# The attention's product with the values in two matmuls for each tile of keys in place of three

## The chip, the cores and the metric

One core of one Trainium2 chip runs one kernel: two layers of a transformer block with sandwiched feed-forward parts and a mixed attention and pooling part, for 256 tokens of an image (x) and 256 tokens of context (ctx), all in float32 arithmetic. The metric is the device time in microseconds of one execution, as the median of several runs; less is better.

## The reference, cut to what matters

```python
def neighbourhood_attention(q, k, v, kc, vc, rpb, rows):      # x's queries
    ...
    scores = jnp.concatenate([s_loc.reshape(...), s_ctx], axis=-1)   # 256 local and 256 context keys
    p = jax.nn.softmax(scores, axis=-1).astype(v.dtype)
    ...
    o = einsum('bhrqkc,brkchd->brqhd', p_loc, v_blk) + einsum('bhrqk,bkhd->brqhd', p_ctx, vc)

def context_attention(q, k, v):                               # ctx's queries, first layer alone
    p = jax.nn.softmax(sc, axis=-1).astype(v.dtype)
    return jnp.einsum('bhqk,bkhd->bqhd', p, v).reshape(b, l, h * dh)

def token_mix(hx, hc, ...):
    ...
    out_x = jnp.concatenate([na_x, pool_x], axis=-1) @ w_out
```

There are 8 heads of 64 channels. In the kernel the local window covers all 256 image tokens (the window of 8 rows is cut to the 4 rows of 64 that there are), with the bias and mask added to the scores. So each head multiplies probabilities of 256 queries by 512 keys with 512 x 64 values, and in the first layer those of 256 context queries by 256 keys with 256 x 64 values.

## The kernel before, in words

**Precision.** Float32 operands of a matmul are held as two parts, a high one in the faster format fp32r and a low one, the rest. `split` (L535) makes them: a ScalarE copy into the high part, and a VectorE subtraction for the low part. `mm3` (L530) multiplies two such pairs with three matmuls: high by high, high by low, low by high.

**Stages.** Each layer is a feed-forward part (ffn), the token mix, and a second feed-forward part. In the token mix, `v_tile` (L957) makes the values of 128 tokens in a PSUM bank (pv) and splits them into V, a tile of 128 tokens by two token tiles by high and low by 512 channels. Keys and queries of a pair of heads come from `k_part` and `q_part`; `roped` turns them (a ScalarE copy, a VectorE shuffle, a GpSimd and a VectorE product with the rotary tables ropet, a VectorE sum, all in a tile rp), and the queries end in qa, the keys in kb. `pooled` is the pooling part, with a chain of GpSimd additions (U, dd) and a product py. The output projection (pd) multiplies mix, the eight blocks of 128 channels from heads and pooling, with the weights w_out; `close` (L784) norms a tile of 128 tokens, adds it to x and turns it into the next part's input.

**One head** (`head`, L1011; pr is the pair, 0 to 3, and e the head in it): scores (pS, and pC for the context's queries), softmax in the tiles sx and sc, transposes of the probabilities into a bank pp, a split into pT (or pT2), and `back` (L1021), which is the change's place. It runs over the tiles of 128 keys, four for x and two for the context. The stationary operand is a 128 x 128 block of V, the high or the low part of both heads of the pair; the moving one is the probabilities' high or low part, 128 keys by 256 queries. The bank po holds 128 channels by 256 queries, of which only the 64 rows of this head are used; `split` brings these to mix's high (mhi) and low (mlo) part. There are 16 such products in layer 0 (8 heads, x and context) and 8 in layer 1.

**Weights.** A stream brings 1 MB pieces by DMA into raw; ScalarE and VectorE split each into two tiles named w (w_big in the profile), one tile ahead of their use.

**Order.** Nothing is written out by hand. The code records its operations, and `Recorder.order` (L293) places them one at a time on five clocks, with prices by `price` (L208), with buffers taken from five pools (16 large slots "big", 10 "wk", 8 PSUM banks, 2 raw, 24 small) and a small bonus for an operation marked with haste. Within an engine the operations then run strictly in the order found. Every changed operation can therefore move all that come after it, on all engines. All recorded operations carry the line of the issuing helper, L376; the profile tells them apart by the names of tiles.

Of the kernel before, what the change touches and what calls it, by code (L numbers as in the profile page):

```python
# [17 lines left out]
P = 128  # L18
D = 1024
KD = D // P  # L20
S = 256
# [372 lines left out]
def tile_dit_block(  # L394
# [25 lines left out]
    nc = rec  # L420
# [530 lines left out]
    def token_mix(l, nxt):  # L951
# [5 lines left out]
        def v_tile(t, wv4):  # L957
            pv = bank("pv")
            tk = slice(t * P, (t + 1) * P)
            for k in range(KD):  # L960
                w = wv4[k // 2]
                hh = H["now"][k // 4]
                c = slice((k % 2) * 512, (k % 2 + 1) * 512)
                mm3(pv, (hh[0][:, k % 4, tk], hh[1][:, k % 4, tk]), (w[:, 0, c], w[:, 1, c]), k == 0, k == KD - 1)
            if t % 2 == 0:
                V[t // 2] = slot([P, 2, 2, 512], "v")
            split(V[t // 2][:, t % 2, 0, :], V[t // 2][:, t % 2, 1, :], pv)

# [42 lines left out]
        def head(pr, e, qk, bx):  # L1011
            qa, kb = qk
            hp = slice(e * 64, (e + 1) * 64)
            vc = slice(pr * P, (pr + 1) * P)
            mhi, mlo = mixed(pr)
# [4 lines left out]

            def back(src, keys, co):  # L1021
                po = bank("po")
                for i, t in enumerate(keys):
                    vt = V[t // 2]
                    mm3(
                        po[:, 0:S],
                        (vt[:, t % 2, 0, vc], vt[:, t % 2, 1, vc]),
                        (src[:, 0, i, :], src[:, 1, i, :]),
                        i == 0,
                        i == len(keys) - 1,  # L1030
                    )
                split(mhi[hp, co], mlo[hp, co], po[hp, 0:S])

# [45 lines left out]
            for t in range(2):  # L1079
# [4 lines left out]
                split(pT[:, 0, :, t * P : (t + 1) * P], pT[:, 1, :, t * P : (t + 1) * P], ppv)  # L1084
            back(pT, (0, 1, 2, 3), XS)
            if full:
                pp = bank("pp")
                for t in range(2):
                    for kt in range(2):
                        o = kt * S + t * P  # L1090
                        nc.tensor.transpose(pp[:, o : o + P], sc[:, t, kt * P : (kt + 1) * P], ident)
                pT2 = wtile([P, 2, 2, S], "pT2", F32R)
                split(pT2[:, 0], pT2[:, 1], pp.rearrange("p (k q) -> p k q", k=2))
                back(pT2, (2, 3), CS)
            rec.haste = 0.0
# [264 lines left out]
```

## Time and profile before

| | |
|---|---|
| median of 3 runs | 1678.48 us (1678.24 to 1678.59) |
| profiled execution | 1679.59 us |
| its span, first to last instruction | 1677.8 us |
| mean granted TensorE clock | 0.994 |
| matmuls of the values' product (po) | 240, in two parts of the span: 455.8 to 569.0 us and 1392.5 to 1468.1 us |

In the profile, PE is TensorE's matmul and PEld its weight load, DVE is VectorE, ACT ScalarE, POOL GpSimd. `out<-in` names the tiles by the program's names. A busy time counts an instruction from its start to its modelled end, so that matmuls in a pipeline overlap. In the timeline, `xN` on a row merges N instructions, and a bracket at its end gives the idle time before it and what ended that. In the chain of waits each row is a stretch of time in which that engine was the one waited for.

### The profile page before, as it was taken

The page shows a single profiled execution, that of the slowest core. Times are in us where ns is not written, and L with a number is a line of the kernel's source. Part 1 is how long each engine was busy: PE and PEld are TensorE (multiplying, and loading weights), DVE is VectorE, ACT ScalarE, POOL GpSimd, SP SyncE. Part 2 cuts the span into 40 slices and gives each one's busy share as a digit, 9 for nine tenths or more (in the row PEclk, how much of TensorE's full clock was granted, in tenths as well). Part 3 has the DMA queues.
Part 4 walks back from the last instruction along what each step waited for, and adds up shares of the span by engine and source line. Part 5 has one row for each costly group of instructions (what it writes and reads, how often), then busy time and mean ns, then how long its engine had stood idle before and what let it go on. Part 6 is the DMA issues. An engine that isn't in the chain of part 4 may idle for free.

```text
span 1677.8 us, 21889 instructions
## 1 busy us (share of the span) xinstructions
PE 1637.7 (98%) x8390; PEld 1374.9 (82%) x8390; DVE 1132.5 (67%) x1610; ACT 689.1 (41%) x1222; POOL 214.7 (13%) x264
## 2 busy tenths in 40 slices
PE   6999999999999999999999999999999999899998
PEld 4988888888877798888888898888888888779997
DVE  7997777556789689867745498533343488975664
ACT  7433222225566562232222273142222367664442
POOL 1022111102133211210110012100000022210000
PEclk9999999999999999999999999999999999999999
DMA  9467656621222426765554248432232212355551
GB/s 373 175 232 247 223 181 210 211 100 60 96 67 93 151 101 211 247 230 204 179 184 163 100 161 302 165 126 88 88 128 97 93 60 98 124 195 195 203 195 58
DMA packets 98953, 269.00 MB, mean 160 GB/s; under 512 B 9425, under 2 KB 39329, under 8 KB 87073
## 3 DMA queue, kind: packets, MB, share of 16 engines
q1 hardware_dynamic: 98848, 267.60, 45.3%
q8 instruction: 66, 1.08, 0.3%
q14 instruction: 39, 0.31, 0.1%
HBM read 251.80 MB, written 1.09 MB: 151 GB/s over the span
## 4 chain that ended last, share of the span: by engine, by line
PE 85%; DVE 5%; ACT 5%; POOL 2%; issue 1%; DMA 1%; SPq 0%; DVEq 0%; POOLq 0%; ACTq 0%
PE pd_ps L376 26%; PE pu_ps L376 25%; PE pg_ps L376 25%; PE pk_ps L376 2%; PE pv_ps L376 2%; ACT n_wk L376 2%; DVE w_big L376 1%; POOL rs_st L376 1%; PE pq_ps L376 1%; DMA w_big<-in_wmod_dram 1%; PE pt_ps L376 1%; ACT w_big L376 1%; PE po_ps L376 1%; ACT sx_wk L376 1%; ACT yg_wk L376 1%
## 5 line engine op out<-in xcount | busy, mean ns | idle before, releaser
L376 DVE TENSOR_TENSOR w_big<-raw_raw,w_big 128x1024 fp32r<-128x1024 f32 x312 | 389.0, 1260 | 167.1 <-ACT w_big L376 166.6
L376 PE MATMUL pu_ps<-h_big,w_big 128*128 128x512 f32 (+1 forms) x2400 | 474.9, 351 | 0.0
L376 PE MATMUL pg_ps<-h_big,w_big 128*128 128x512 f32 (+1 forms) x2208 | 439.8, 353 | 1.4 <-ACT h_big L376 1.4
L376 PEld LDWEIGHTS pu_ps<-h_big,w_big 128*128 128x128 f32 x2400 | 389.8, 188 | 62.2
L376 PE MATMUL pd_ps<-w_big,g_big 128*128 128x512 f32 x1848 | 431.2, 394 | 0.0
L376 ACT ACTIVATE w_big<-raw_raw 128x1024 fp32r<-128x1024 f32 x312 | 322.3, 1053 | 261.1 <-PE pd_ps L376 95.3
L376 PEld LDWEIGHTS pg_ps<-h_big,w_big 128*128 128x128 f32 x2208 | 361.4, 189 | 61.1 <-ACT h_big L376 1.8
L376 PEld LDWEIGHTS pd_ps<-w_big,g_big 128*128 128x128 f32 x1848 | 346.3, 188 | 78.9
L376 DVE SCALAR_TENSOR_TENSOR acc_wk<-wm_wk,csil,acc_wk 128x1024 f32<-128x1024 f32 x196 | 247.0, 1293 | 42.2 <-DMA wm_wk<-in_wmod_dram 42.0
L376 ACT ACTIVATE g_big<-tt_wk 128x512 fp32r<-128x512 f32 (+1 forms) x84 | 49.1, 585 | 314.3 <-DVE tt_wk L376 314.2
L376 POOL TENSOR_TENSOR part_wk<-part_wk 128x512 f32<-128x512 f32 (+2 forms) x84 | 93.4, 1113 | 504.8 <-DMA part_wk<-acc_wk 405.9
L376 ACT ACTIVATE tt_wk<-pg_ps 128x512 f32<-128x512 f32 (+1 forms) x86 | 47.3, 550 | 163.0 <-PE pg_ps L376 134.3
L376 DVE TENSOR_TENSOR tt_wk<-tt_wk,pu_ps 128x512 f32<-128x512 f32 (+1 forms) x86 | 54.0, 628 | 77.2 <-PE pu_ps L376 76.8
L376 POOL TENSOR_SCALAR rs_st<-sq_st 128x1 f32<-128x1 f32 x24 | 7.6, 315 | 731.9 <-ACT n_wk L376 731.8
L376 DVE SCALAR_TENSOR_TENSOR tt_wk<-tt_wk,pg_ps 128x512 f32<-128x512 f32 (+1 forms) x86 | 53.9, 627 | 69.5 <-ACT tt_wk L376 69.1
L376 DVE TENSOR_TENSOR g_big<-tt_wk,g_big 128x512 fp32r<-128x512 f32 (+1 forms) x84 | 54.1, 644 | 30.7 <-ACT g_big L376 30.7
L376 PE MATMUL pd_ps<-w_big,mix_big 128*128 128x512 f32 x288 | 71.8, 398 | 0.5 <-DVE mix_big L376 0.5
L376 DVE TENSOR_TENSOR y_big<-y_big,pd_ps 128x512 f32<-128x512 f32 x56 | 37.7, 683 | 45.1 <-PE pd_ps L376 45.0
L376 PEld LDWEIGHTS pd_ps<-w_big,mix_big 128*128 128x128 f32 x288 | 52.9, 190 | 12.1 <-DVE mix_big L376 1.2
L376 PE MATMUL pk_ps<-h_big,w_big 128*128 128x512 f32 (+1 forms) x240 | 50.0, 350 | 0.0
L376 PE MATMUL pv_ps<-w_big,h_big 128*128 128x512 f32 x192 | 47.0, 397 | 0.0
L376 PEld LDWEIGHTS pk_ps<-h_big,w_big 128*128 128x128 f32 x240 | 37.7, 188 | 5.1
(136 smaller groups left out, 1219.1 us busy)
## 6 DMA issues: line engine op xcount, KB each, us to landing
raw_raw<-in_wgu_dram SPq DMA_DIRECT2D x84, 1024.0 KB, 4.9
wm_wk<-in_wmod_dram SPq DMA_DIRECT2D x128, 512.0 KB, 6.5
raw_raw<-in_wdn_dram SPq DMA_DIRECT2D x44, 1024.0 KB, 5.0
part_wk<-acc_wk SPq DMA_DIRECT2D x224, 64.0 KB, 2.5
raw_raw<-in_wkq_dram SPq DMA_DIRECT2D x8, 1024.0 KB, 4.9
raw_raw<-in_wout_dram SPq DMA_DIRECT2D x8, 1024.0 KB, 4.8
w_big<-in_wmod_dram SPq DMA_DIRECT2D x7, 1024.0 KB, 11.7
gb_wk<-grow SPq DMA_DIRECT2D x10, 512.0 KB, 5.4
```

The costliest lines, as they stand in the source:

```text
L376: getattr(getattr(nc, op.engine), op.method)(*[self.real(a) for a in op.args], **{k: self.real(a) for k, a in op.kw.items()})
```

## The change

V's tile gets another layout: for each token tile and each pair of heads four blocks of 64 channels, in the order high part of head 0, low of head 0, low of head 1, high of head 1. The two blocks of one head are now side by side and serve as one stationary operand of 128 columns. One matmul with the probabilities' high part and one with their low part then give the high part's product in 64 rows of po and the low part's product in the other 64; both halves of the bank are used, and the product of low by low, left out before, is included. For head 0 the high block lies in rows 0 to 63, for head 1 in rows 64 to 127, which are the rows of the head in mix.

The two halves have to be added. ScalarE copies the high half of po to mhi, as before, and the other half to a work area tmp, across the partitions; VectorE subtracts mhi from po's high half into tmp in place of mlo; GpSimd adds the two pieces of tmp into mlo. The work area is the head's own sx or sc, whose probabilities have been transposed by then; it stays taken until that add.

```diff
-                V[t // 2] = slot([P, 2, 2, 512], "v")
-            split(V[t // 2][:, t % 2, 0, :], V[t // 2][:, t % 2, 1, :], pv)
+                V[t // 2] = slot([P, 2, 4, 4, 64], "v")
+            vt = V[t // 2][:, t % 2]
+            split(vt[:, :, 0:4:3, :], vt[:, :, 1:3, :], pv.rearrange("p (r e d) -> p r e d", r=4, e=2))
...
-            def back(src, keys, co):
+            def back(src, keys, co, tmp):
+
                 po = bank("po")
                 for i, t in enumerate(keys):
-                    vt = V[t // 2]
-                    mm3(
-                        po[:, 0:S],
-                        (vt[:, t % 2, 0, vc], vt[:, t % 2, 1, vc]),
-                        (src[:, 0, i, :], src[:, 1, i, :]),
-                        i == 0,
-                        i == len(keys) - 1,
-                    )
-                split(mhi[hp, co], mlo[hp, co], po[hp, 0:S])
+                    vt = V[t // 2][:, t % 2, pr, 2 * e : 2 * e + 2, :].rearrange("p b d -> p (b d)")
+                    for part in range(2):
+                        mm(po[:, 0:S], vt, src[:, part, i, :], i == 0 and part == 0, i == len(keys) - 1 and part == 1)
+                nc.scalar.activation(mhi[hp, co], po[hp, 0:S], AF.Copy)
+                nc.scalar.activation(tmp[hp, 0:S], po[HEADS[1 - e], 0:S], AF.Copy)
+                nc.vector.tensor_sub(tmp[hp, S : 2 * S], po[hp, 0:S], mhi[hp, co])
+                nc.gpsimd.tensor_add(mlo[hp, co], tmp[hp, 0:S], tmp[hp, S : 2 * S])
...
-            back(pT, (0, 1, 2, 3), XS)
+            back(pT, (0, 1, 2, 3), XS, sx[:, 0, :])
...
-                back(pT2, (2, 3), CS)
+                back(pT2, (2, 3), CS, sc.rearrange("p t c -> p (t c)"))
```

The planner's order stays the same up to the first product po, and differs from there to the end. Three places matter below. The numbers in the names count the recorded tiles and differ between the two programs.

First, TensorE in layer 0, the products for x of pair 2 (pu is the pooling part's input, taken in between). Before, with the last eleven matmuls of head 0 (po_ps_4367) and all twelve of head 1 (po_ps_4403):

```order
L376 MATMUL po_ps_4367<-pT_big_4349,v_big_3512 128x256 x5
L376 MATMUL po_ps_4367<-pT_big_4349,v_big_3307 128x256 x6
L376 MATMUL po_ps_4403<-pT_big_4380,v_big_3512 128x256
L376 MATMUL pu_ps_4320<-h_big_3137,w_big_4151 128x512
L376 MATMUL pu_ps_4320<-h_big_3119,w_big_4151 128x512
L376 MATMUL pu_ps_4320<-h_big_3134,w_big_4151 128x512
L376 MATMUL po_ps_4403<-pT_big_4380,v_big_3512 128x256 x5
L376 MATMUL po_ps_4403<-pT_big_4380,v_big_3307 128x256 x6
```

and now, head 1 alone:

```order
L376 MATMUL po_ps_4437<-pT_big_4416,v_big_3512 128x256
L376 MATMUL pu_ps_4379<-h_big_3137,w_big_4197 128x512
L376 MATMUL pu_ps_4379<-h_big_3119,w_big_4197 128x512
L376 MATMUL pu_ps_4379<-h_big_3134,w_big_4197 128x512
L376 MATMUL pu_ps_4379<-h_big_3119,w_big_4197 128x512 x2
L376 MATMUL po_ps_4437<-pT_big_4416,v_big_3512 128x256 x3
L376 MATMUL po_ps_4437<-pT_big_4416,v_big_3307 128x256 x4
```

One head's product has twelve matmuls before and eight now.

Second, TensorE in layer 0 just ahead of the first scores pS of head pair 3. Before, the rest of a pooling input (pu) and a first matmul of the context's scores stand there, and the output projection pd begins after all the scores:

```order
L376 MATMUL pu_ps_4459<-h_big_3134,w_big_4214 128x512
L376 MATMUL pu_ps_4459<-h_big_3119,w_big_4214 128x512
L376 MATMUL pC_ps_4511<-kb_big_3922,qa_wk_4405 128x256
L376 MATMUL pS_ps_4514<-kb_big_3922,qa_wk_4405 128x512 x2
L376 MATMUL pS_ps_4517<-kb_big_3922,qa_wk_4405 128x512 x2
L376 MATMUL pS_ps_4526<-kb_big_3922,qa_wk_4405 128x512 x2
L376 MATMUL pS_ps_4530<-kb_big_3922,qa_wk_4405 128x512 x2
L376 MATMUL pC_ps_4511<-kb_big_3922,qa_wk_4405 128x256 x3
L376 MATMUL pd_ps_4548<-w_big_4413,mix_big_3967 128x512 x3
```

and now:

```order
L376 MATMUL pu_ps_4379<-h_big_3119,w_big_4197 128x512
L376 MATMUL pC_ps_4479<-kb_big_3940,qa_wk_4290 128x256 x4
L376 MATMUL pd_ps_4490<-w_big_4435,mix_big_3949 128x512 x3
L376 MATMUL pd_ps_4498<-w_big_4435,mix_big_3949 128x512 x3
L376 MATMUL pd_ps_4506<-w_big_4435,mix_big_3949 128x512 x3
L376 MATMUL pd_ps_4511<-w_big_4435,mix_big_3949 128x512 x3
L376 MATMUL pd_ps_4490<-w_big_4449,mix_big_3949 128x512 x3
L376 MATMUL pd_ps_4498<-w_big_4449,mix_big_3949 128x512 x3
L376 MATMUL pd_ps_4506<-w_big_4449,mix_big_3949 128x512 x3
L376 MATMUL pS_ps_4539<-kb_big_3940,qa_wk_4290 128x512 x2
L376 MATMUL pd_ps_4511<-w_big_4449,mix_big_3949 128x512 x3
L376 MATMUL py_ps_4559<-ds_wk_4556,wp_wk_3357 128x512
```

Twenty-one matmuls of pd have moved ahead of the scores (the pooling input is finished earlier), and the scores come in pieces with pd and py between them.

Third, GpSimd in layer 0 around the rotary product of pair 3's queries, the row rp<-rp,ropet in the middle (rp_wk_4454 before, rp_wk_4465 now); dd and U are pooling additions, bound for pair 2's block of the pooling part. Before:

```order
L376 TENSOR_TENSOR rp_wk_4227<-rp_wk_4227,ropet 128x256
L376 MEMSET U_wk_4309 128x592
L376 TENSOR_TENSOR rp_wk_4454<-rp_wk_4454,ropet 128x256
L376 TENSOR_TENSOR dd_wk_4470<-U_wk_4309 128x591
L376 TENSOR_TENSOR dd_wk_4485<-dd_wk_4470 128x589
L376 TENSOR_TENSOR dd_wk_4470<-dd_wk_4485 128x585
L376 TENSOR_TENSOR dd_wk_4485<-dd_wk_4470,U_wk_4309 128x256 x2
```

and now:

```order
L376 MEMSET U_wk_4369 128x592
L376 TENSOR_TENSOR mix_big_4241<-sc_wk_4269 64x256
L376 TENSOR_TENSOR mix_big_4241<-sx_wk_4263 64x256
L376 TENSOR_TENSOR dd_wk_4453<-U_wk_4369 128x591
L376 TENSOR_TENSOR dd_wk_4470<-dd_wk_4453 128x589
L376 TENSOR_TENSOR mix_big_4241<-sx_wk_4281 64x256
L376 TENSOR_TENSOR rp_wk_4465<-rp_wk_4465,ropet 128x256
L376 TENSOR_TENSOR dd_wk_4453<-dd_wk_4470 128x585
L376 TENSOR_TENSOR dd_wk_4470<-dd_wk_4453,U_wk_4369 128x256 x2
```

The rotary product came ahead of the pooling additions; it now stands behind two of them and behind three of the new adds into mix.

More of the change, by code (lines that the diff above doesn't have):

```diff
@@ L1013, in head @@
             hp = slice(e * 64, (e + 1) * 64)
-            vc = slice(pr * P, (pr + 1) * P)
             mhi, mlo = mixed(pr)
```

## The prediction

> **What bounds the kernel now.** The first view is the page's table of busy time. Its TensorE row says where to start:
>
> ```profile
> PE 1637.7 (98%) x8390; PEld 1374.9 (82%) x8390; DVE 1132.5 (67%) x1610; ACT 689.1 (41%) x1222; POOL 214.7 (13%) x264
> ```
>
> TensorE is busy for 98% of the span, so a matmul less should be time less. That is an average, though, and the change touches only the two attention parts. The second view is the busy time in stretches: us from the start, length, then busy us of PE, PEld, DVE, ACT and POOL, the granted TensorE clock, DMA share, GB/s. Layer 0's heads run from 448 to 569 and its output projection to 592; layer 1's heads run from 1383 to 1468.
>
> ```profile
> 448.00:484.00 36.00, 35.69 (x190) 29.41 (x188) 28.00 (x77) 22.33 (x63) 7.99 (x11) 1.00 0.23 79
> 484.00:519.70 35.70, 34.44 (x188) 28.90 (x189) 31.99 (x93) 24.23 (x66) 8.27 (x10) 1.00 0.15 46
> 519.70:530.00 10.30, 10.30 (x69) 9.28 (x68) 9.37 (x22) 9.77 (x24) 0.00 (x0) 1.00 0.40 142
> 530.00:541.40 11.40, 7.56 (x36) 6.00 (x34) 11.21 (x14) 5.26 (x10) 8.61 (x7) 0.92 0.28 93
> 541.40:545.50 4.10, 4.06 (x11) 3.35 (x12) 3.43 (x8) 1.96 (x5) 1.88 (x3) 0.50 0.84 296
> 545.50:550.00 4.50, 4.50 (x21) 3.37 (x20) 4.04 (x10) 4.03 (x11) 2.11 (x1) 0.89 0.02 5
> 550.00:557.00 7.00, 4.99 (x27) 3.36 (x25) 6.97 (x12) 4.59 (x12) 6.69 (x6) 1.00 0.41 150
> 557.00:569.00 12.00, 12.00 (x75) 10.66 (x74) 8.36 (x22) 8.26 (x19) 1.80 (x3) 1.00 0.51 175
> 569.00:592.00 23.00, 23.00 (x102) 18.44 (x101) 10.35 (x12) 8.89 (x18) 1.73 (x4) 1.00 0.38 137
> 1383.00:1409.00 26.00, 24.44 (x161) 21.69 (x159) 20.71 (x54) 17.03 (x40) 8.14 (x10) 1.00 0.23 83
> 1409.00:1430.00 21.00, 20.47 (x129) 18.20 (x130) 18.66 (x50) 15.09 (x39) 4.64 (x7) 1.00 0.28 102
> 1430.00:1457.00 27.00, 22.82 (x142) 19.20 (x142) 25.44 (x70) 18.86 (x51) 11.26 (x14) 1.00 0.33 120
> 1457.00:1468.00 11.00, 11.00 (x71) 9.86 (x70) 9.58 (x17) 8.91 (x17) 0.00 (x0) 1.00 0.47 174
> ```
>
> Layer 0 falls into three pieces. From 448 to 530 and from 557 on, TensorE is nearly full. From 530 to 557 VectorE is the full one (25.65 of 27.0 us) and TensorE stands still for some 6 us. In layer 1, 1430 to 1457 is VectorE's (25.44 of 27), and TensorE lacks 4.2 us there. The third view, the waits of TensorE, names the largest hole, and the timeline shows it with what follows:
>
> ```profile
> PE pS_ps L376 <- DVE qa_wk L376: 3.9, 1, 3.9
> 541.44 3.75 PE L376 MATMUL pS_ps<-kb_big,qa_wk 128*128 128x512 f32 x8 [3.88 <-DVE qa_wk L376]
> ```
>
> The scores of head pair 3 (pS) wait for that pair's queries (qa), which VectorE makes late. The eight matmuls then take 3.75 us at a clock of 0.50. So the attention is bound by turns, and the question is how much of the removed TensorE work lies where TensorE is last.
>
> **What goes.** The values' product (po) before, and its two evictions:
>
> ```profile
> L376 PE MATMUL po_ps<-pT_big,v_big x192: 274/282/386, 458.2 to 1467.8; 128*128 128x256 f32 x192
> L376 PE MATMUL po_ps<-pT_wk,v_big x48: 276/280/384, 455.8 to 565.7; 128*128 128x256 f32 x48
> L376 ACT ACTIVATE mix_big<-po_ps x24: 360/378/382, 457.8 to 1468.1; 64x256 fp32r<-64x256 f32 x24
> L376 DVE TENSOR_TENSOR mix_big<-po_ps,mix_big x24: 404/422/429, 458.6 to 1468.5; 64x256 fp32r<-64x256 f32 x24
> ```
>
> A third of 240 goes: 80, of which 48 in layer 0 (8 heads x 6 tiles of keys) and 32 in layer 1. The 282 ns is a latency; the chain of waits gives the rate, and how much of the chain is po at all:
>
> ```profile
> by line: PE pk_ps L376 11.8%; PE pq_ps L376 9.7%; PE po_ps L376 7.3%; DVE w_big L376 7.2%; PE pp_ps L376 6.5%; issue 6.3%; PE pS_ps L376 6.1%; PE pd_ps L376 6.1%; ACT sx_wk L376 4.7%; ACT w_big L376 3.2%; DVE sm_st L376 3.0%; DVE sc_st L376
> by line: PE pd_ps L376 12.0%; PE pk_ps L376 11.2%; issue 8.1%; DVE w_big L376 8.0%; DVE sm_st L376 6.7%; ACT sx_wk L376 6.5%; DVE rp_wk L376 5.7%; DVE sx_wk L376 4.9%; DVE kb_big L376 4.8%; DVE pT_big L376 3.4%; PE po_ps L376 3.2%; ACT kb_b
> 467.29 0.38 ACT mix_big L376
> 567.69 1.32 PE po_ps L376 x11
> 569.01 23.02 PE pd_ps L376 x99
> 1395.34 0.33 ACT mix_big L376
> ```
>
> The two long rows are the chain's shares from 448 to 570 and from 1383 to 1470. Eleven po in 1.32 us is 0.12 us each, so the 80 are 9.6 us of TensorE (5.8 in layer 0, 3.8 in layer 1): the ceiling if no hole changes. On the chain po has 7.3% of 122 us (8.9 us) and 3.2% of 87 us (2.8 us); a third of these is **-3.0 us** in layer 0 and **-0.9 us** in layer 1.
>
> **What moves.** The planner places everything anew. In layer 0 the last po is followed by 99 matmuls of the output projection (pd) in a row, at 23.02/99 = 0.2325 us each; in the new order by 82, since 21 pd stand ahead of pair 3's scores, where TensorE stood. Seventeen fewer after the last po are **-3.95 us** for any given time of that po. The 21 are 4.9 us of work in a hole of 3.88, so the spell at half clock should shrink; only part of its 4.1 us was lost to VectorE, which was busy 3.43 of them: **-0.5** (0 to -2). The new order also has places in pair 3 where po waits for its own transposes behind two or four matmuls only; before, TensorE lacked 2.0 us in 550 to 557 for the same reason. I add **+0.5** (0 to 1.9).
>
> In layer 1 the last po is followed by 38 pd in place of 39 and 3, but the first token tile is complete 13 matmuls after it, not 11, and its closing chain (norm, transposes, next layer's input) sets the end there:
>
> ```profile
> 1478.00:1481.90 3.90, 1.29 (x9) 0.81 (x7) 3.87 (x8) 3.80 (x10) 0.86 (x2) 0.98 0.61 248
> 1481.90:1486.00 4.10, 4.05 (x11) 3.25 (x12) 4.08 (x5) 3.32 (x6) 1.44 (x1) 0.61 0.02 6
> ...
> 1481.94 1.22 PE L376 MATMUL pg_ps<-w_big,h_big 128*128 128x512 f32 x2 [2.65 <-ACT h_big L376]
> ```
>
> TensorE is busy 1.29 of 3.90 us, so two pd later is **+0.5**, and the four pd saved buy nothing. po off the chain that joins it in 1383 to 1430 gives **-0.5** (0 to -1.9: 48 x 1/3 x 0.12).
>
> After such holes the clock is 0.50 and 0.61 for about four us. The Trainium skill (TensorE: Matmul & The Clock Gate, What's actually happening) puts the drop to half clock after an idle window of about 3.4 us. By that a hole kept under 3.4 us would cost no clock, and the spell in layer 0 would vanish whole, for -2 instead of -0.5. The trace agrees only in part: in layer 1 no single wait was longer than 2.65 us, and the clock fell all the same; so I keep the smaller gain.
>
> **What comes.** Each of the 24 evictions gets a second ScalarE copy from PSUM and a GpSimd add; VectorE's subtraction only changes its target. The copy has no row yet: it crosses from one half of the partitions to the other. I take the first copy's 0.378 us, the nearest row; its ends are nothing and all 24 on the path (9.1 us). ScalarE is 66 and 70% busy in the two parts (80.4 of 121 us, 59.9 of 85); of the first copies one stands on layer 1's chain (1395.34) and three on layer 0's (467.29 is the first), so **+1.0** and **+0.35**. The stored V differs in address only; its eviction is taken at nothing.
>
> The add lengthens the way to the low half of mix by about 0.8 us. At the end of layer 1 the first matmul that reads it stands eleven behind the last po (2.5 us), against 0.38 + 0.42 + 0.74; in layer 0 dozens of pd lie between. It hides, unless GpSimd is late. Its price and its harm:
>
> ```profile
> L376 POOL TENSOR_TENSOR rp_wk<-rp_wk,ropet x16: 730/741/1310, 434.7 to 1433.1; 128x256 f32<-128x256 f32 x16
> L376 DVE TENSOR_TENSOR w_big<-raw_raw,w_big 128x1024 fp32r<-128x1024 f32 x28 | 37.1, 1334 | 6.1 <-ACT w_big L376 5.8
> 532.04 1.23 DVE L376 TENSOR_TENSOR w_big<-raw_raw,w_big 128x1024 fp32r<-128x1024 f32 x1
> 535.08 3.40 POOL L376 TENSOR_TENSOR dd_wk<-dd_wk 128x589 f32<-128x589 f32 x2
> 535.27 2.19 DVE L376 TENSOR_TENSOR w_big<-raw_raw,w_big 128x1024 fp32r<-128x1024 f32 x1
> ...
> L376 DVE TENSOR_TENSOR rp_wk<-rp_wk x16: 404/424/1376, 436.1 to 1437.3; 128x256 f32<-128x256 f32 x16
> L376 DVE TENSOR_TENSOR rp_wk<-rp_wk 128x256 f32<-128x256 f32 x8 | 4.3, 539 | 0.3
> ```
>
> Twenty-four adds at 0.74 (up to 1.31) are 17.8 us. VectorE's weight subtraction takes 1.23 us alone and 2.19 beside GpSimd's additions. Over the 28 of 395 to 625 the excess is 28 x 0.104 = 2.9 us, and GpSimd was busy 39.1 us from 448 to 592 (the sum of the rows above): 0.075 us of VectorE per us of GpSimd. The rotary sum, 424 ns at the median and 539 on average in the same window, adds 8 x 0.115 = 0.9 us: 3.8/39.1, or about 0.10. So 16 adds cost **+1.2** and 8 cost **+0.6**, between nothing and all 17.8 us. The Trainium skill (SBUF — State Buffer, Who interferes with whom) says that a VectorE instruction with two SBUF inputs and a GpSimd one that reads SBUF exclude each other for a whole instruction. By that each add that meets such an operation costs up to its full 0.74 us; the 2.19 us row agrees, and it speaks against the change. The new subtraction has one input in PSUM, so by the page it is not itself a victim.
>
> On GpSimd's queue the rotary multiply of pair 3's queries now stands behind two long additions and an add that waits for VectorE:
>
> ```profile
> L376 DVE STREAM_SHUFFLE rp_wk<-rp_wk x16: 441/448/452, 434.7 to 1436.3; 128x256 f32<-128x256 f32 x16
> 533.29 0.69 DVE L376 TENSOR_REDUCE sc_st<-pC_ps 128x2 f32<-128x512 f32 x1
> L376 DVE TENSOR_TENSOR rp_wk<-rp_wk,ropet x16: 406/420/985, 435.3 to 1436.8; 128x256 f32<-128x256 f32 x16
> ```
>
> From that add's subtraction to the rotary sum VectorE has this shuffle, reduction and product and a weight subtraction (1.23) to do, 2.8 us, which cover GpSimd's 0.74 + 0.74. Uncovered, up to 1.5 us would land on pair 3's scores.
>
> Sum: layer 0: -3.95 - 3.0 - 0.5 + 0.5 + 1.0 + 1.2 = -4.75; layer 1: -0.9 + 0.5 - 0.5 + 0.35 + 0.6 = +0.05. Together -4.7 us. The profiled execution took 1679.59 us (span 1677.8), 1.1 above the median of the runs; -4.7 gives 1674.9 there and 1678.48 - 4.7 = **1673.8 us** at the median.
>
> **The rivals.** *A, TensorE is last throughout:* no hole grows, all 9.6 us come through, the costs hide: 1668.9. For it: 98%, and 34.44 of 35.7. Against it: 25.65 of 27.0 on VectorE.
>
> *B, VectorE paces both parts:* removed products on the chain are replaced by the VectorE work just behind them (-3.0, -0.9, -0.5 and -0.5 vanish), the rest stays: -3.95 + 0.5 + 1.0 + 1.2 + 0.5 + 0.35 + 0.6 = +0.2, so 1678.7. For it: 85% busy on VectorE even in TensorE's stretch 448 to 530.
>
> *C, slower: the adds block VectorE where it is full* (530 to 557, 1430 to 1457), above all before pair 3's scores. With all other terms -6.5, it decides from 6.5/0.74 = 9 adds that hold it whole; 13 give +3.1: 1681.6. For it: 2.19 against 1.23. Against it: most adds fall outside these stretches.
>
> That the change doesn't do what it says is excluded by the new order: four po per product of two tiles in place of six.
>
> **How the numbers follow.** The forecast holds about 1671 to 1676.5 (the ends of the half clock, of the bare waits and of the copies) and gets 0.51; A 0.15, B 0.20, C 0.14. Faster by over 0.2% (3.4 us, what a measurement here can tell from no change; under 1675.1) is A and 0.37 of the forecast: 0.52. Within 0.2% are the forecast's other 0.14 and B: 0.34. Slower is C: 0.14. The range runs from A's time to C's, 1668.9 to 1681.6, leaving out half of each, some 0.15.
>
> **What would show it.** Right: po x160 at the same 0.28 us; the last po of layer 0 near 567, followed by 82 pd without a hole; pair 3's scores at a clock over 0.5. Wrong: VectorE over 97% busy in longer stretches with TensorE's holes grown (B), or w_big well over 1.4 us on average there and qa the longest wait (C).

## The result, and the profile after

The changed kernel takes 1689.07 us (median of 6 runs, 1687.26 to 1690.40) against 1678.53 us of the kernel before, measured beside it (6 runs, 1678.24 to 1680.23). The ratio is 1.006, with a 95% interval of 1.0047 to 1.0073: slower by 0.6%, some 10 us. The forecast was 4.7 us faster, and the time lies outside its range. The profiled execution took 1688.76 us (span 1687.0, mean TensorE clock 0.990).

The busy times and the rows of po answer to those shown of before. First the page, then the groups of the tile po:

```profile
PE 1638.5 (97%) x8310; PEld 1368.6 (81%) x8310; DVE 1138.2 (67%) x1610; ACT 699.2 (41%) x1246; POOL 231.3 (14%) x288
```

```profile
L376 PE MATMUL po_ps<-pT_big,v_big x128: 274/280/388, 457.9 to 1475.0; 128*128 128x256 f32 x128
L376 PE MATMUL po_ps<-pT_wk,v_big x32: 276/281/386, 455.2 to 577.6; 128*128 128x256 f32 x32
L376 ACT ACTIVATE mix_big<-po_ps x24: 359/378/382, 457.1 to 1475.3; 64x256 fp32r<-64x256 f32 x24
L376 ACT ACTIVATE sx_wk<-po_ps x16: 375/378/382, 460.2 to 1475.7; 64x256 f32<-64x256 f32 x16
  POOL mix_big L376: 63.8, 13
```

The 80 matmuls are gone (x128 and x32), each as long as before, and a copy across the halves costs the same 378 ns as a straight one. The last po of each layer is later all the same: 577.6 against 568.7 us, and 1475.0 against 1467.8. The last row is from the list of those that waited for a po product's eviction: GpSimd, 13 times, 63.8 us in all. Its adds are placed where it has to wait for VectorE.

To find the loss, take the start of six matmuls that both programs have, and compare the stretches between them (us):

| from, to | before | after | difference |
|---|---|---|---|
| layer 0: first pS to pair 3's first pS | 93.5 | 97.6 | +4.1 |
| to the last po | 27.3 | 32.8 | +5.5 |
| to the last pd on mix | 34.9 | 31.0 | -3.9 |
| to layer 1's last po | 864.2 | 866.3 | +2.1 |
| to the first pg of the last ffn | 14.2 | 15.8 | +1.6 |
| all the rest | 643.8 | 643.5 | -0.3 |

Those waits of TensorE that grew or are new (before, the first two were 5.7 and 4.0 us in all and the others were not there), and the stretches around pair 3 (columns as in the prediction), show where it stands:

```profile
PE pS_ps L376 <- DVE qa_wk L376: 6.5, 3, 4.5
PE pg_ps L376 <- ACT h_big L376: 6.4, 2, 5.0
PE pu_ps L376 <- DVE w_big L376: 3.8, 1, 3.8
PE pd_ps L376 <- DVE sx_wk L376: 1.9, 1, 1.9
```

```profile
541.00:557.00 16.00, 10.79 (x28) 6.90 (x28) 11.87 (x22) 8.81 (x21) 6.91 (x6) 0.68 0.46 164
557.00:569.00 12.00, 8.18 (x34) 5.91 (x34) 10.11 (x21) 7.76 (x20) 9.86 (x9) 0.88 0.31 112
569.00:592.00 23.00, 22.66 (x108) 18.24 (x107) 12.79 (x17) 12.38 (x23) 1.92 (x4) 0.99 0.48 171
1430.00:1457.00 27.00, 22.37 (x145) 20.36 (x144) 26.21 (x64) 20.27 (x49) 9.35 (x13) 0.94 0.18 61
```

From 541 to 569 TensorE is idle for 9.0 of 28 us, and part of the rest is at half clock. From 557 to 569 it was full before (12.00). The timeline tells the story in order:

```profile
532.85 3.88 DVE L376 TENSOR_TENSOR w_big<-raw_raw,w_big 128x1024 fp32r<-128x1024 f32 x2
533.61 0.39 ACT L376 ACTIVATE rp_wk<-pq_ps 128x256 f32<-128x256 f32 x1
533.62 2.03 POOL L376 TENSOR_TENSOR dd_wk<-dd_wk 128x589 f32<-128x589 f32 x1
...
536.76 0.43 DVE L376 TENSOR_TENSOR sx_wk<-po_ps,mix_big 64x256 f32<-64x256 f32 x1
...
537.23 0.45 DVE L376 STREAM_SHUFFLE rp_wk<-rp_wk 128x256 f32<-128x256 f32 x1
...
537.34 0.74 POOL L376 TENSOR_TENSOR mix_big<-sx_wk 64x256 fp32r<-64x256 f32 x1 [1.69 <-DVE sx_wk L376]
...
538.15 0.73 POOL L376 TENSOR_TENSOR rp_wk<-rp_wk,ropet 128x256 f32<-128x256 f32 x1
...
541.26 0.94 DVE L376 TENSOR_TENSOR rp_wk<-rp_wk 128x256 f32<-128x256 f32 x1
...
544.88 0.70 PE L376 MATMUL pS_ps<-kb_big,qa_wk 128*128 128x512 f32 x2 [4.50 <-DVE qa_wk L376]
...
547.19 1.18 PE L376 MATMUL pS_ps<-kb_big,qa_wk 128*128 128x512 f32 x2
...
550.92 4.64 PE L376 MATMUL pd_ps<-w_big,mix_big 128*128 128x512 f32 x10 [0.78 <-ACT mix_big L376]
...
555.35 0.84 PE L376 MATMUL pp_ps<-ident,sc_wk 128*128 128x128 f32 x4
...
556.50 0.63 PE L376 MATMUL pS_ps<-kb_big,qa_wk 128*128 128x512 f32 x2
...
560.75 0.73 PE L376 MATMUL pS_ps<-kb_big,qa_wk 128*128 128x512 f32 x2 [0.24 <-DVE pT_big L376]
```

Two things went another way than forecast. The queries are late: the scores start at 544.88, not at 541.44, and the hole before them is 4.50 us, although 21 pd now stand ahead of it. And the eight scores, one block of 3.75 us before, are spread over 16 us: the second head's stand at 556.50 and 560.75. The output projection's matmuls that were moved ahead write to four PSUM banks (two tiles of 128 tokens, two halves each) of the eight (PLACES), and hold them to the end. The planner places a score only where it has a free bank (`room` in `Recorder.order`), and here ten pd and four transposes stand ahead of the second head's first score.

The +2.1 of the fourth row has no such place. It grows little by little through the two feed-forward parts, in which TensorE waits for 1.2 us in all (0.9 before), and is complete before layer 1's first score. Its cause stays open.

### The profile page after: what moved, and what is told of

The parts are those of the page before. It is cut to its first block, busy times and chain, and to the rows that moved or that the text cites. A ratio compares the mean times of both kernels' runs of the same rounds, so it can differ in the third digit from the quotient of the medians.

```text
span 1687.0 us, 21820 instructions
## 1 busy us (share of the span) xinstructions
PE 1638.5 (97%) x8310; PEld 1368.6 (81%) x8310; DVE 1138.2 (67%) x1610; ACT 699.2 (41%) x1246; POOL 231.3 (14%) x288
## 5 line engine op out<-in xcount | busy, mean ns | idle before, releaser
L376 PE MATMUL pd_ps<-w_big,mix_big 128*128 128x512 f32 x288 | 76.3, 415 | 3.3 <-DVE sx_wk L376 1.9
```

The source lines that it names most:

```text
L376: getattr(getattr(nc, op.engine), op.method)(*[self.real(a) for a in op.args], **{k: self.real(a) for k, a in op.kw.items()})
```

## The experiments

All times below are medians beside the kernel before on the same chip; differences are taken from the ratio (0.01% is 0.17 us), since the kernel before itself came out between 1678.5 and 1679.7 us from one group of runs to the next.

### First: the order or the work?

Theory O puts the loss on the planner's new order, theory W on the added copies and adds. The planner moves everything, so order and work had to be separated: a recorded operation gets a field `real`, the order is found with the planned operation, and what stands in `real` is issued in its place.

```diff
-            getattr(getattr(nc, op.engine), op.method)(
...
+            for engine, method, args, kw in [(op.engine, op.method, op.args, op.kw)] if op.real is None else op.real:
...
+                    one.real = [("tensor", "matmul", (po[:, 0:S], vb, ph), dict(start=a, stop=False))]
+                    two.real = [("tensor", "matmul", (po[:, 0:S], vb, pl), dict(start=False, stop=z))]
+                    three.real = []
+                c, s = split(mhi[hp, co], mlo[hp, co], po[hp, 0:S])
+                far = mlo[hp, co]
+                c.real = [(c.engine, c.method, c.args, c.kw), ("scalar", "activation", (tmp[hp], po[HEADS[1 - e], 0:S], AF.Copy), {})]
+                s.real = [
+                    ("vector", "tensor_sub", (far, po[hp, 0:S], mhi[hp, co]), {}),
+                    ("gpsimd", "tensor_add", (mlo[hp, co], tmp[hp], far), {}),
+                ]
```

**Old order, new work:** 

> The changed kernel's work in the old kernel's order: the order is planned with the old operations, and then each third po matmul is left out, the two others get the new operands, and the second ScalarE copy and the GpSimd add are issued right behind the copy and the subtraction that they belong to. The add works in place on mix's low half, with one small work area, so no large buffer is held longer. Theory O (the order: the planner now starts the output projection ahead of pair 3's scores, and its four PSUM banks keep the second head's scores out): the old order has no such trap, so most of the 9.6 us of removed matmuls comes through against small costs, 1669 to 1676 us. Theory W (the added work: second copies and GpSimd adds hold ScalarE, VectorE and po's banks): the same added work is here, so it stays slower than before, 1683 to 1690 us.

**New order, old work** (the changed kernel, with three matmuls in `two.real` and an empty `real` for the second copy and the add): 

> The other corner: the changed kernel's order with the old kernel's work. The order is planned with the new operations, and then three matmuls of the old kind are issued where two stand, the second copy and the GpSimd add are left out, and the subtraction goes straight to mix's low half. Theory O: the loss is the order's, so this is slower than before by as much as the changed kernel or more, 1688 to 1698 us. Theory W: without the added work the loss is gone and the 80 matmuls are back, 1676 to 1683 us.

**New order with a rule:**

```diff
+        for d in self.behind:
+            after.setdefault(d, False)
...
                 scores(pS[t], t * P, ALL)
+                last[0] = rec.ops[-1]
...
+            rec.behind = [last[0]] if full else []
             for j in range(4):
```

> The changed kernel with one rule for the planner: in layer 0 no matmul of the first output projection products (pd) may be placed before the last scores (pS) of pair 3. Nothing else is touched; the instructions are the same in number and kind. Theory O: the 9.6 us that TensorE loses more than before between 530 and 592 us mostly come back, 1677 to 1683 us, with all four pairs of pS in one go again and no late scores near 556 and 561. Theory W: the order there is a consequence and no cause; within 2 us of the changed kernel, 1687 to 1691 us.

**Old order, two matmuls and nothing added** (no `c.real`, no `s.real`): 

> As the first kernel, in the old order, but without the second copy and without the GpSimd add; the subtraction writes mix's low half as before. It leaves out the product of the values' low part. It shows what the 80 matmuls are worth alone, and the difference to the first kernel is the price of the added work where nothing else moves. Theory O: 1668 to 1674 us, and the first kernel 0 to 4 us above it. Theory W: 1668 to 1674 us as well, and the first kernel 10 us or more above it.

| order | work | time | ratio (95%) | to before |
|---|---|---|---|---|
| old | old | 1679.73 | 1 | 0 |
| old | new | 1687.78 | 1.0051 (1.0038 to 1.0063) | +8.6 |
| old | two matmuls alone | 1676.60 | 0.9986 (0.9977 to 0.9995) | -2.4 |
| new | old | 1687.59 | 1.0049 (1.0035 to 1.0062) | +8.2 |
| new, with the rule | new | 1686.24 | 1.0042 (1.0029 to 1.0054) | +7.1 |
| new | new | 1689.07 | 1.0060 (1.0047 to 1.0073) | +10.1 |

Neither theory holds alone. The work costs 8.6 us where nothing is reordered, so theory O, which said 1669 to 1676, falls; the order costs 8.2 us with the work unchanged, so theory W, which said 1676 to 1683, falls too. They don't add: together 10.1. Each order was planned for its own work, so in both crossed kernels a part of the price may be that the order doesn't fit the work.

Where the time goes tells more than the sums. The stretches of the result's table again, as differences to the kernel before (profiled executions, us; that of the last column is 1.8 us over its median):

| from, to | new order, new work | new order, old work | old order, new work |
|---|---|---|---|
| layer 0: first pS to pair 3's first pS | +4.1 | +2.7 | +2.4 |
| to the last po | +5.5 | +4.1 | +0.5 |
| to the last pd on mix | -3.9 | -3.9 | +0.3 |
| to layer 1's last po | +2.1 | +2.2 | +3.5 |
| to the first pg of the last ffn | +1.6 | +1.6 | +1.1 |
| all the rest | -0.3 | +1.3 | +2.0 |

The changed kernel loses where its order loses with the old work, and 1.4 us more in each of the first two stretches. The 8.6 us of the old order lie elsewhere in part: its 3.5 of the fourth row are in layer 1's heads, where the changed kernel loses 0.2.

The rule does what it was made for: the eight scores stand within 4.0 us again, and from pair 3's first score to the last po it is 27.9 us in place of 32.8. But its place behind the last po is given up for that (34.6 us to the last pd, not 31.0), so layer 0 gains 1.4 us in all; theory O had said 1677 to 1683 us. The other 2.0 us come between layer 0's last pd and layer 1's first score: 779.5 us, as before, not 781.5. All four kernels in whose order pd stand ahead of pair 3's scores and the scores are apart take 781.4 to 781.7 us there, and all others 779.5 to 779.8. What stays is the first stretch, 97.4 us, with the wait now bare:

```profile
PE pS_ps L379 <- DVE qa_wk L379: 11.3, 3, 9.3
```

So the early pd did not make the queries late; they had filled half of a hole of 9.3 us.

Of 9.6 us of matmuls only 2.4 come through even with nothing added (both theories had said 1668 to 1674 us): TensorE waits longer for what VectorE makes, for the queries 5.2 and 2.8 us in the two parts in place of 3.9 and 1.8. VectorE itself isn't full, though. Before the change its instructions cover 103 us of the 121 from 448 to 569 us, and 74 of the 85 from 1383 to 1468 us; its waits there add up to 14.6 and 9.9 us, most of them for ScalarE. The longest group of each part:

```profile
DVE sc_st L376 <- ACT sc_wk L376: 4.1, 3, 2.6
```

```profile
DVE sm_st L376 <- ACT sx_wk L376: 4.6, 4, 2.1
```

VectorE and ScalarE hand the work to each other, and their common pace hides most of what TensorE saves. That this pace alone sets the 2.4 us, and not also an order planned for three matmuls, is likely but not shown.

### Second: which part of the added work?

The old order again, with one piece of the added work at a time. Theory C: the copy. Theory G: the GpSimd add.

**The copy alone** (the line of the add left out): 

> The old order, two matmuls, and of the added work the second ScalarE copy alone; the GpSimd add is left out, so the low part's product is copied and not used. The two kernels around it are measured: without either 1676.6 us, with both 1687.8 us. Theory C (the copy is the price: ScalarE is 95 to 98% busy from 520 to 530 us and VectorE behind it from there, so most of 24 x 0.38 = 9.1 us is on the path): 1683 to 1687 us. Theory G (the GpSimd add is the price: it holds VectorE's two-input operations and stands in GpSimd's queue): 1675 to 1679 us.

**The add alone** (the copy left out, tmp filled with zeros once): 

> The other half: the old order, two matmuls, and of the added work the GpSimd add alone, of a work area of zeros; the second copy, and with it the low part's product, is left out. Theory C: 1675 to 1680 us. Theory G: 1683 to 1688 us. If each costs about half (5 to 6 us, 1680 to 1683 us, in both kernels), neither theory holds alone.

**The add on VectorE** (`"vector"` for `"gpsimd"`): 

> The old order with the whole added work, but the add of the two halves on VectorE in place of GpSimd. Theory G, because GpSimd blocks VectorE: the blocking goes and an add of 0.4 us on VectorE comes, faster than with the GpSimd add, 1680 to 1685 us. Theory C, with VectorE and ScalarE pacing the attention: 24 more operations on a full engine, 1688 to 1697 us.

**Two matmuls planned anew** (the second copy and the add taken out of the changed kernel, the subtraction to mlo): 

> The changed kernel planned anew without the second copy and without the GpSimd add (it leaves out the product of the values' low part): two matmuls, nothing added, and the planner is free to use it. In the old order the same work gave 1676.6 us. If the old order alone kept the gain small, a new order gives more of the 9.6 us: 1668 to 1673 us. If VectorE and ScalarE pace the attention, no order does: 1675 to 1679 us. If the planner's order by itself is a risk of several us either way, as the old work in the new order showed (1687.6 us), it can also be slower than the old kernel: 1680 to 1688 us.

| work | time | ratio (95%) | to before | VectorE, sum in both parts |
|---|---|---|---|---|
| two matmuls alone | 1676.60 | 0.9986 (0.9977 to 0.9995) | -2.4 | 198.7 |
| and the copy | 1681.55 | 1.0015 (1.0006 to 1.0024) | +2.5 | 199.3 |
| and the add | 1686.94 | 1.0050 (1.0036 to 1.0063) | +8.4 | 206.4 |
| and both | 1687.78 | 1.0051 (1.0038 to 1.0063) | +8.6 | 205.0 |
| and the copy, add on VectorE | 1688.10 | 1.0057 (1.0045 to 1.0070) | +9.6 | 208.8 |
| two matmuls, planned anew | 1680.77 | 1.0010 (1.0001 to 1.0019) | +1.7 | 198.5 |

The last column adds up the durations of VectorE's instructions in the two parts (198.7 before). Neighbours overlap by some 0.08 us, which it counts twice, so it says how much longer instructions run and not how full the engine is: in the last kernel it is 84.0 us in layer 1's stretch of 81.7 us.

Twenty-four copies cost 4.9 us, about half of their 9.1 us; they leave VectorE's sum as it was. Twenty-four adds cost 10.8 us alone and 6.1 beside the copies, and they lengthen VectorE's sum by 7.7 us. On GpSimd they cost as much as on VectorE itself: that run came out at theory C's 1688, not at G's 1680 to 1685, so GpSimd saved nothing. For the rest theory G holds for the larger part, with C's half of the copies beside it. The two matmuls alone planned anew are 4.1 us slower than in the old order (1.0010 against 0.9986); there, too, pair 3's eight scores stand 13.4 us apart.

How an add that VectorE doesn't wait for lengthens VectorE's sum is seen in the timelines. The kernel without adds:

```profile
553.80 3.68 POOL L378 TENSOR_TENSOR dd_wk<-dd_wk,U_wk 128x256 f32<-128x256 f32 x4
...
557.33 0.17 DVE L378 TENSOR_TENSOR sm_st<-sm_st 128x2 f32<-128x2 f32 x1
```

The same place with the add alone:

```profile
556.18 0.73 POOL L378 TENSOR_TENSOR mix_big<-tmp,mix_big 64x256 fp32r<-64x256 f32 x1 [1.49 <-DVE mix_big L378]
...
556.87 2.83 POOL L378 TENSOR_TENSOR dd_wk<-dd_wk,U_wk 128x256 f32<-128x256 f32 x4
...
558.30 1.43 DVE L378 TENSOR_TENSOR sm_st<-sm_st 128x2 f32<-128x2 f32 x1
```

The add waits 1.49 us for VectorE, and the four operations of the pooling chain (dd) behind it start at 556.87, not 553.80; the stretch as a whole is 1.0 us later by then. They now lie on an operation of VectorE with 2 columns, which takes 1.43 us in place of 0.17 and is on the way to the next exponential. Measured against the same operations' median length, VectorE's excess beside GpSimd grows from 14.7 to 22.5 us in the two parts; of the 7.8 us only 2.3 lie beside an add itself, and most of the rest beside dd (12.9 to 15.6) and the fills of U (0.1 to 2.4).

### Third: the add's reading, its number, and the planner

**Fills in place of adds** (two `memset` of mlo[hp, co] in place of the add): 

> As the kernel with the GpSimd add alone (1686.9 us; without the add 1676.6 us), but in place of each add two GpSimd fills with zeros of the same 64 x 256 piece of mix's low half. They wait for the same VectorE subtraction, stand at the same place of GpSimd's queue, take about as long together and are waited for by the same matmuls, but they read nothing; the low half of the heads' part of mix is left out. Theory L (the add's reads hold up VectorE: in the kernel with the add VectorE's operations of the two attention parts sum up to 7.7 us more, all of it in small operations beside an add): 1676 to 1680 us. Theory Q (the wait in GpSimd's queue, ahead of the rotary products and the pooling chain, or the later low half, is the price): 1683 to 1688 us.

**One add for both heads of a pair:**

```diff
+    tmp = fixed([P, N_TOK], "tmp", BF16)
...
+                ] + [("gpsimd", "tensor_add", (mlo[:, co], tmp[:, co], mlo[:, co]), {})] * e
```

> The old order with the whole added work, but one GpSimd add for both heads of a pair (128 x 256 in place of two of 64 x 256), issued behind the second head's subtraction; the work area holds the other half in bf16, with room for x and context. Twelve adds in place of 24, each about as long. Theory L: about half of the 6.2 us that the adds cost beside the copies goes: 1683 to 1686 us. If an add costs by its bytes or is hidden, nothing moves: 1687 to 1689 us.

**The same planned anew, with the rule:**

```diff
-                nc.scalar.activation(tmp[hp, 0:S], po[HEADS[1 - e], 0:S], AF.Copy)
-                nc.vector.tensor_sub(tmp[hp, S : 2 * S], po[hp, 0:S], mhi[hp, co])
-                nc.gpsimd.tensor_add(mlo[hp, co], tmp[hp, 0:S], tmp[hp, S : 2 * S])
+                nc.scalar.activation(tmp[hp, co], po[HEADS[1 - e], 0:S], AF.Copy)
+                nc.vector.tensor_sub(mlo[hp, co], po[hp, 0:S], mhi[hp, co])
+                if e == 1:
+                    nc.gpsimd.tensor_add(mlo[:, co], tmp[:, co], mlo[:, co])
```

> The best whole version that the runs so far point to, planned anew: one GpSimd add for both heads of a pair, the work area of its own (no sx or sc held until the add), and the rule that no pd may be placed before pair 3's scores. By parts: the changed kernel 1689.1, the rule -2.8, half of the adds -3: about 1683 us, 1680 to 1686. Faster than the old kernel only if the planner's new order happens to be a good one, since the second copies alone (5 us) cost more than the matmuls bring (3.1 us).

**The old kernel with another price for po:**

```diff
+            if outs[0].buf.name == "po":
+                return 0.073
```

> The old kernel, its work unchanged to the last instruction, with one number of the planner's changed: it takes a po matmul for 0.073 us in place of 0.11, as if a third of po's time were gone. Only the order can differ. If orders of the planner are all about as good, 1677 to 1681 us. If any change draws an order that is several us better or worse, as the old work in the changed kernel's order (1687.6 us) and the two matmuls planned anew (1680.8 us against 1676.6 us) suggest, it comes out 3 to 10 us away, more likely above.

| kernel | time | ratio (95%) | to before |
|---|---|---|---|
| fills in place of adds | 1684.39 | 1.0030 (1.0019 to 1.0042) | +5.0 |
| one add per pair, old order | 1684.45 | 1.0031 (1.0020 to 1.0042) | +5.2 |
| one add per pair, planned anew, rule | 1683.32 | 1.0023 (1.0014 to 1.0032) | +3.9 |
| old work, po priced at 0.073 | 1683.96 | 1.0029 (1.0017 to 1.0040) | +4.9 |

Theory L, that the add's reads are the price, falls for the larger part: fills that read nothing still cost 7.4 us over the two matmuls, of the adds' 10.8. VectorE's sum tells why: 204.3, 5.6 more. In layer 1 the shifted pooling chain meets a weight subtraction that takes 1.2 us alone:

```profile
1449.32 0.67 POOL L378 MEMSET mix_big<- 64x256 f32 x2 [1.47 <-DVE mix_big L378]
1449.95 0.73 POOL L378 TENSOR_TENSOR dd_wk<-dd_wk,U_wk 128x256 f32<-128x256 f32 x1
1450.12 3.69 DVE L378 TENSOR_TENSOR w_big<-raw_raw,w_big 128x1024 fp32r<-128x1024 f32 x1
1450.65 0.72 POOL L378 TENSOR_TENSOR dd_wk<-U_wk 128x319 f32<-128x319 f32 x1
1451.32 0.74 POOL L378 TENSOR_TENSOR dd_wk<-dd_wk,U_wk 128x256 f32<-128x256 f32 x1
1452.02 0.71 POOL L378 TENSOR_TENSOR dd_wk<-dd_wk 128x317 f32<-128x317 f32 x1
```

The subtraction ends 1.1 us after the last of four dd.

Half as many adds cost 2.7 us over the copies in place of 6.1, as expected (their work area is in bf16, which was not tried by itself; the copies into it take 380 ns as before). Planned anew with the rule, that version came out as forecast too, and not evenly: layer 0 takes 151.9 us from the first score to the last pd on mix, against 155.6 before, while the way to layer 1's last po gives 1.4 us back, the stretch behind it 1.8 and all the rest 2.2. That is why the change was tried in layer 0 alone. The last row of the table is a warning for all the others: the old work in an order that the planner drew with one other price, too low for that work, is 4.9 us slower. Again pd stand ahead of pair 3's scores, and the scores are apart (12.9 us).

### Fourth: the wait in the queue, or the time; and layer 0 alone

**Adds of 2 columns** (`far[:, 0:2]` and a tmp of 2 columns in the kernel with the add alone): 

> As the kernel with the GpSimd add alone (1686.9 us; without it 1676.6 us), but each add covers 2 columns in place of 256, so that it waits for the same subtraction at the same place of GpSimd's queue and is short; the low part's product is left out. Theory Q (the wait in the queue is the price): 1682 to 1687 us. Theory T (the time for which the add keeps GpSimd busy, and with it VectorE, directly or through the pooling chain that it pushes back): 1676 to 1680 us.

**The change in layer 0 alone** (the pair version with the rule; `if not full` takes the old values' layout, mm3 and split): 

> The best whole version (one add for both heads of a pair, its own work area, the rule for pd) in layer 0 alone; layer 1 has the old values' layout, three matmuls and the old eviction. That version took 152.0 us from layer 0's first scores to its last output projection, against 155.7 before, and 101.8 us against 98.8 from layer 1's first scores to the next part's first matmul. With layer 0's gain and layer 1 as before: about 1675 us. With an unlucky order in layer 1, as the planner draws it anew: 1678 to 1683 us.

The tiny adds give 1679.12 us, ratio 1.0000 (0.9991 to 1.0009): 2.4 us over the two matmuls, where the full adds cost 10.8. They wait as long (the groups of the two kernels from 440 to 1480 us: busy us, mean ns, then the idle time before them):

```profile
L378 POOL TENSOR_TENSOR mix_big<-tmp,mix_big 64x256 fp32r<-64x256 f32 x24 | 20.5, 856 | 70.2 <-DVE mix_big L378 65.5 <-DVE sm_st L378 4.4
```

```profile
L378 POOL TENSOR_TENSOR mix_big<-tmp,mix_big 64x2 fp32r<-64x2 f32 x24 | 7.5, 313 | 76.5 <-DVE mix_big L378 71.2 <-DVE sm_st L378 5.2
```

So theory T holds for three quarters: what costs most is the time for which GpSimd is kept busy, 13 us more of it, with what that pushes back, and not the wait in its queue.

Layer 0 alone gives 1676.04 us, ratio 0.9982 (0.9973 to 0.9991): 3.0 us faster than before and 13 faster than the change as it was made. From the first score to the last pd on mix layer 0 takes 151.9 us (before 155.6, changed 161.3); the part from the last pd to the end is as before. The scores of pair 3 stand in one block:

```profile
539.83 3.75 PE L379 MATMUL pS_ps<-kb_big,qa_wk 128*128 128x512 f32 x8 [5.66 <-DVE qa_wk L379]
```

The wait for the queries is still the longest of the attention, now with 36 matmuls less ahead of it (48 in the layer); it ends when VectorE has made them. In the 3.0 us there is a good draw of the order: layer 0 takes 151.9 us with all of the added work, and 153.7 in the old order with the two matmuls alone. How much of the gain is the change's own was not separated.

## Why the prediction was wrong, point by point

**What bounds the kernel: half right.** "The attention is bound by turns" was the reading, with TensorE nearly full from 448 to 530 us and VectorE from 530 to 557. The turns are there, but work taken out of TensorE's busy stretches mostly became waiting: of the 9.6 us of matmuls 2.4 came through with all costs taken away, in the old order. The terms for po on and beside the chain (-3.0, -0.9, -0.5) were of the right kind and too large by 2.0 together; rival B (VectorE paces) was nearer, though VectorE paces together with ScalarE.

**Seventeen pd fewer behind the last po, -3.95: the step that failed.** The stretch behind the last po is shorter by 3.9 us, as worked out. "For any given time of that po" was the error: with the pd moved ahead, in four of eight banks, the second head's scores came 10 and 13 us later behind the first score, and the last po 5.5 us later within its stretch. In place of -3.95 the two stretches give +1.6. The rule of the third kernel undoes both and nets 1.4 us in layer 0 (and 2.0 behind it). The rule shows that the early pd are the cause; that it is by their banks follows from the planner's code, and no run changed the number of banks.

**The copies and the adds, +3.15: the second step that failed, by size.** In the old order, where no pd moves, the change still costs 8.6 us, so the sign would have been wrong without the first error too. The two terms are taken up below.

**The half clock, -0.5, and the bare waits, +0.5.** The hole did not shrink: 4.50 us against 3.88, followed by 4.1 us at a clock of 0.58:

```profile
544.90:549.00 4.10, 3.54 (x9) 1.82 (x9) 4.03 (x10) 2.46 (x6) 1.02 (x2) 0.58 0.90 296
```

Filling a hole from TensorE's side does nothing to the engine that ends it. The bare waits were sized from the old trace (up to 1.9); with the scores apart, TensorE lacked 9.0 us between 541 and 569, of which 3.9 belong to the hole before the scores and 5.1 are such waits.

**Layer 1's closing chain, +0.5: right in kind, too small.** It is +1.6. The old work in the new order has 15.7 us there as well, with the same wait: the longest before the last part's first pg went from 2.65 to 5.0 us in both. The new work in the old order has 15.3 us by another way, with a wait of 0.8 us for a GpSimd add.

**The copies, +1.35: too small.** They cost 4.9 us in the old order, 0.20 each. The chain of waits named only four copies on it. The rest were priced at nothing because they were off that one chain; with VectorE waiting for ScalarE as it does here, that is no reason, but which of the copies cost was not looked for one by one.

**The adds, +1.8: the largest miss of a size.** Beside the copies they cost 6.1 us, alone 10.8. The price of 0.10 us of VectorE for each us of GpSimd came from weight subtractions and rotary sums alone. Measured it is 7.7 us for 20.5, or 0.38. The excess that was looked for in large operations lies as much in those of 2 columns, and in the pooling chain that the adds push back. The mark of rival C was a w_big well over 1.4 us on average in the full stretches. It tells nothing: from 530 to 557 us the mean was 1.62 before and 1.55 after, from 1430 to 1457 us 1.31 and 1.42. Rival C (1681.6, 0.14) was right that GpSimd's work holds VectorE, and wrong in where and how much: it counted the adds themselves and 3.1 us.

**GpSimd's queue before pair 3's queries.** It was not what made them late: the rotary product of GpSimd, 0.73 us from 538.15, is over long before VectorE's rotary sum at 541.26. The kernel before has the first steps of these queries earlier:

```profile
532.04 0.39 ACT L376 ACTIVATE rp_wk<-pq_ps 128x256 f32<-128x256 f32 x1 [1.49 <-DVE qa_wk L376]
...
533.91 0.45 DVE L376 STREAM_SHUFFLE rp_wk<-rp_wk 128x256 f32<-128x256 f32 x1
```

Of the 4.1 us, 2.2 have arisen before the ScalarE copy (533.61 now, and the first score lies 0.6 us earlier). From the copy to VectorE's shuffle it is 3.6 us in place of 1.9, as two weight subtractions stand ahead of the shuffle and take 3.88 us beside dd. From the shuffle to the scores it is 7.7 us and was 7.5.

**Sum.** In the old order: -2.4 (matmuls), +4.9 (copies), +6.1 (adds), +8.6 in all, where the forecast's terms were -4.4, +1.35 and +1.8; the new order brings it to +10.1. The forecast's terms for the new order were -3.95, -0.5, +0.5 and +0.5, a gain of 3.45. Measured, the order costs 1.5 us with the new work and 8.2 with the old. Whichever is taken first, both were forecast as gains and came out as losses.

## What to carry to other kernels

Before work is taken from the engine with the highest busy share, look in the stretch that the change touches at the engines that feed it: here VectorE and ScalarE wait for each other, and a quarter of the removed matmul time came through. A sum of durations is no measure of how full an engine is, since neighbours overlap; its growth shows which instructions run longer. A helper engine beside a busy one is no free place: the adds cost as much on GpSimd as on VectorE, by their time and by what they push back, and half as many cost 2.7 us in place of 6.1. And where a greedy planner draws the order, separate order from work (old order with new work, new order with old work), compare the two stretch by stretch before a cause is named, and look at what early work holds, PSUM banks above all.

## What the runs showed of the hardware

VectorE operations of 2 columns, 0.15 to 0.17 us alone, took up to 1.43 us beside GpSimd's work, more than a weight subtraction of 1024 columns alone (1.2 us); size doesn't protect. Fills hold one kind of them too, in the kernel with tiny adds:

```profile
515.91 0.58 POOL L378 MEMSET U_wk<- 128x592 f32 x1
516.02 0.50 DVE L378 TENSOR_SCALAR sm_st<-sm_st 128x2 f32<-128x2 f32 x1
```

The Trainium skill (SBUF — State Buffer, Who interferes with whom) states, beside the rule for two inputs that the prediction used, that copies, casts and tensor_scalar in a two-port mode and GpSimd exclude each other, whichever was issued first. The row agrees: a TENSOR_SCALAR of 0.15 us ended with the fill. The prediction read only the first half of that rule, and so took the small operations and the fills for harmless.

A TENSOR_TENSOR of two SBUF inputs isn't held by a fill. In the kernel with the change in layer 0 alone both kinds lie beside one:

```profile
479.80 0.59 POOL L379 MEMSET U_wk<- 128x592 f32 x1
...
479.96 0.16 DVE L379 TENSOR_TENSOR sm_st<-sm_st 128x2 f32<-128x2 f32 x1
...
480.16 0.26 DVE L379 TENSOR_SCALAR sm_st<-sm_st 128x2 f32<-128x2 f32 x1
```

The first keeps its 0.16 us, the second ends with the fill. And the new subtraction, which reads po from PSUM, takes 0.40 to 0.43 us in all of its 24 places in the changed kernel, beside GpSimd's work or not.
